# Late modulation columns queued behind their own round's weights, in a transformer kernel on one core

## The chip, the core and the metric

The kernel is one program on one core of a Trainium2 chip. Its engines are TensorE (PE in the profile: matrix products, with PEld for its weight loads), VectorE (DVE), ScalarE (ACT), GpSimd (POOL) and SyncE (SP), which here only issues transfers. Each engine takes its instructions in the order in which they were written into its program; semaphores make it wait for others. The metric is the device time of one execution in microseconds (us); lower is better.

## The reference, cut to what matters

Two transformer blocks run one after the other on 256 tokens of width 1024, all in fp32. The first block ends in a layer that picks among 16,384 single-neuron experts; the second has retention, a Fourier branch and two feed-forward layers. The second block scales and shifts its activations by vectors that come from a small input through one large matrix:

```
mod_x = (silu(c) @ w_ada[l] + b_ada[l])[:, None, :]          # 9 x 1024 outputs, K = 1024
mod_c = (silu(c_ctx) @ w_ada[l] + b_ada[l])[None, None, :]   # the same matrix, another input
...
a = gelu(einsum('bqhkd,bqd->bqhk', peer_u[expert], hb))      # first block: the expert layer
return einsum('bqhk,bqhkd->bqd', g * a, peer_v[expert])
```

In the kernel the expert layer is computed dense: all 128 groups of 128 experts, with a gate that is zero where an expert is not picked.

## The kernel before, in words

Activations lie with the 1024 features in eight chunks of 128 partitions and the 256 tokens along the row. A weight tile is 128x1024 fp32 (512 KB). For fp32 accuracy each tile is split into a high part `wh` (a cast by ACT) and a low part `wl` (a subtraction by DVE, both in `split`, lines 104 and 105), and each product is made of three matmuls (`mm3`, lines 115 to 117).

**The expert stage** is the loop over `i` from 0 to 127, called rounds here. A round does three things. `up(i + 2)` loads a tile of `peer_u`, splits it, multiplies it with `h2` (24 matmuls into `ua`), applies gelu on ACT (`fs`, line 844), multiplies with the gates on DVE (`fs`, line 845) and splits the result into `zh` and `zl` (`two`). `acc_rows` loads a tile of `peer_v`, splits it, and adds 24 matmuls into the accumulators `va`. Then the round may hand out late modulation columns, below. So a clean round is 48 matmuls on PE, two casts and two small operations on ACT, and two `wl` and two small operations on DVE.

The buffers set how far ahead the work runs: four for a loaded tile (`raw`), three each for `wh` and `wl`. `raw_tile` (line 79) issues each load on SP and keeps it in `tmp["dma"]`; `split` keeps its DVE subtraction in `tmp["lo"]`. At the end of a round both are those of the round's `peer_v` tile.

**The late modulation columns** are the 56 tiles of `w_ada_2` that hold outputs 16 to 71 (in chunks of 128) of `mod_x`, 24 of which are wanted for `mod_c` too. `gemv2_late` loads each tile into one of two slots of `gx` and makes a dot product along the row on DVE: one product with `cb2`, and for the 24 tiles a second with `gx[:, 0]`, 80 in all. After every four columns a tiny DVE addition puts the bias on. The generator is pulled in rounds 18 and later by

```
while late and done[0] * 98 < 80 * (i - 17) and next(late, 0) is None:
    pass
```

so that the source has the 80 products spread over rounds 18 to about 115. At round 116 the memory of `gx` is taken over by `hc`.

**What sets the order.** The source order is not the order in the engines' programs: a scheduler places each engine's instructions by its own estimate of when their inputs are ready. Nothing ties a column's load or product to the round that handed it out. `tc.issue_after(ins)` is the tool for that: what is written inside it, as far as it is on the engine of `ins`, is placed behind `ins` in that engine's program; it adds no wait. The kernel uses it elsewhere, as in `some`.

Of the kernel before, what the change touches and what calls it, by code (L numbers as in the profile page):

```python
# [17 lines left out]
OP = mybir.AluOpType  # L18
# [24 lines left out]
def block_kernel(ctx: ExitStack, tc: tile.TileContext, I, out):  # L43
    nc = tc.nc
    V, S, T = nc.vector, nc.scalar, nc.tensor
# [6 lines left out]
    tmp = {"gr": None, "side": 0, "first": 4, "b": 4}  # L52
# [11 lines left out]
    def col(name, i=0, n=1):  # L64
        o, _ = _COLS[name]
        return cols[:, o + i:o + i + n]
# [13 lines left out]
    def raw_tile(src, pool=None):  # L80
        r = (pool or tmp["ws"]).tile([128, 1024], FT, name="raw", tag="raw", bufs=4 if pool else tmp["raw"])
        tmp["dma"] = nc.sync.dma_start(r, src)
        return r
# [236 lines left out]
    def gemv2_late(gx):  # L320

        both, alone = iter(range(16, 40)), iter(range(40, 72))
        for n in range(56):
            i, outs = (next(both), 2) if n % 2 and n < 48 else (next(alone), 1)
            r = gx[:, 2 + n % 2]
            nc.sync.dma_start(r, I["w_ada_2"][i - 16])
            for k, (v, m) in enumerate(((cb2, modx), (gx[:, 0], modc))[:outs]):
                V.scalar_tensor_tensor(r if k == outs - 1 else tmp["gs"], r, 1.0, v, op0=OP.mult, op1=OP.mult,
                                       accum_out=m[:, i:i + 1])
                done[0] += 1  # L330
            if i % 4 == 3:
                s = slice(i - 3, i + 1)
                for m in (modx, modc)[:outs]:
                    V.tensor_add(m[:, s], m[:, s], col("b_ada_2", i - 3, 4))
            yield
# [250 lines left out]
    for c in range(4):  # L586
# [4 lines left out]
        for e in range(2):  # L591
            r = slice(64 * e, 64 * e + 64)
# [256 lines left out]
    with tc.issue_after(tmp["spill"].ins):  # L849
        nc.sync.dma_start(cb2, I["c2"][:, 0])  # L850
        S.activation(cb2, cb2, AF.Silu)
        zs = [up(0), up(1)]
        late = None
        for i in range(128):
            if i < 126:
                zs.append(up(i + 2))
            acc_rows(acc, [I["peer_v"][i]], [zs.pop(0)], i == 0, i == 127)
            if i == 17:

                gx = cr.tile([128, 4, 1024], FT, name="gx", tag="g0")  # L860
                nc.sync.dma_start(gx[:, 0], I["c2"][:, 1])
                S.activation(gx[:, 0], gx[:, 0], AF.Silu)
                tmp["gs"] = gx[:, 1]
                late = gemv2_late(gx)

            while late and done[0] * 98 < 80 * (i - 17) and next(late, 0) is None:
                pass
            if i == 116:
                hch = cr.tile([128, 16, 256], FR, name="hc", tag="g0")
                hch, hcl = hch[:, 0:8], hch[:, 8:16]  # L870
                for k in (0, 4):
                    r = raw_tile(hc_d[:, k:k + 4]).rearrange("p (a b) -> p a b", a=4)
                    split(r, hch[:, k:k + 4], hcl[:, k:k + 4])
                zch = cr.tile([128, 2 * (NF - NFA), 256], FR, name="zc", tag="g1")
                zch, zcl = zch[:, 0:NF - NFA], zch[:, NF - NFA:]
# [415 lines left out]
```

## Time and profile before

| what | value |
|---|---|
| median of 3 runs | 2127.04 us (2125.74 to 2132.92) |
| profiled execution, its own time | 2117.54 us |
| span of the profiled execution, first to last instruction | 2115.6 us |
| mean granted TensorE clock over the span | 0.982 |
| PE busy | 2031.5 us (96%) |
| DVE busy | 1444.3 us (68%) |
| ACT busy | 1050.7 us (50%) |
| HBM read | 403.11 MB |

A matmul record has a start that is taken and an end that is modelled, and matmuls overlap in the pipeline; so "PE busy" hides short gaps, and the number of matmuls that start in a stretch says more about its pace. The expert stage runs from 505.2 us (first `ua` matmul) to 1220 us.

### The profile page before, as it was taken

What the parts mean: (1) busy time and instruction counts of PE and PEld (TensorE: products, weight loads), DVE (VectorE), ACT (ScalarE), POOL (GpSimd) and SP (SyncE); (2) the same over time, 40 slices, a digit from 0 to 9 for tenths busy, and PEclk for the clock granted to TensorE, in tenths of its full rate; (3) what the DMA queues carried; (4) which work ended last, traced back from release to release, by engine and by line L of the source; (5) the groups of instructions that cost most, each with busy time, mean ns of one, the idle gap of its engine ahead of it and who ended that gap; (6) DMA issues with size and microseconds to landing.
All of it is one profiled execution on the core that took longest, in us unless ns stands there. A gap on an engine that the chain in (4) does not pass through costs nothing.

```text
span 2115.6 us, 40439 instructions
## 1 busy us (share of the span) xinstructions
PE 2031.5 (96%) x16326; PEld 1940.6 (92%) x16326; DVE 1444.3 (68%) x2680; ACT 1050.7 (50%) x1745; POOL 136.3 (6%) x92
## 2 busy tenths in 40 slices
PE   6999997899999999999999999999999999999998
PEld 3987897788999999999999999999989899989998
DVE  6876989797589988655556566546734676665555
ACT  3444543498554444454445557534534544444443
POOL 1000176400000000000000000000000000010000
PEclk8999998999999999999999999999999999999999
DMA  9857543214588887655555665534456654434553
GB/s 340 320 175 249 196 154 120 90 41 148 194 288 315 309 290 264 204 192 197 191 198 195 210 233 181 197 112 145 168 182 214 204 175 160 150 137 151 192 196 114
DMA packets 115562, 412.02 MB, mean 195 GB/s; under 512 B 12848, under 2 KB 14384, under 8 KB 114864
## 3 DMA queue, kind: packets, MB, share of 16 engines
q1 hardware_dynamic: 111392, 395.82, 54.2%
q0 software_dynamic: 3696, 13.11, 1.8%
q8 instruction: 128, 2.10, 0.4%
q10 hardware_dynamic: 288, 0.52, 0.1%
q14 instruction: 58, 0.48, 0.1%
HBM read 403.11 MB, written 6.29 MB: 194 GB/s over the span
## 4 chain that ended last, share of the span: by engine, by line
PE 68%; DVE 4%; DMA 3%; ACT 2%; issue 2%; POOL 0%; DVEq 0%; SPq 0%; ACTq 0%; POOLq 0%
PE va L117 5%; PE mm L117 5%; PE va L116 5%; PE ua L117 5%; PE mm L116 5%; PE mm L115 4%; PE ua L115 4%; PE ua L116 4%; PE va L115 4%; PE fu L116 4%; PE fu L115 4%; PE fu L117 4%; DMA gx<-w_ada_dram 3%; PE fa L116 2%; PE fa L117 2%; PE fa L115 2%
## 5 line engine op out<-in xcount | busy, mean ns | idle before, releaser
L105 DVE TENSOR_TENSOR wl<-raw,wh 128x1024 fp32r<-128x1024 f32 x578 | 709.0, 1229 | 493.4 <-ACT wh L104 492.1
L104 ACT CAST wh<-raw 128x1024 fp32r<-128x1024 f32 x614 | 643.5, 1051 | 759.2 <-issue 356.6
L117 PE MATMUL ua<-hh,wl 128*128 128x256 f32 x1024 | 284.3, 278 | 3.6 <-DVE wl L105 3.6
L115 PE MATMUL ua<-hh,wh 128*128 128x256 f32 x1024 | 283.4, 277 | 0.6 <-ACT fs L844 0.3
L116 PE MATMUL ua<-hh,wh 128*128 128x256 f32 x1024 | 283.2, 277 | 0.0
L116 PE MATMUL va<-zl,wh 128*128 128x256 f32 x1024 | 277.8, 278 | 2.9 <-DVE zl L105 2.9
L117 PE MATMUL va<-zh,wl 128*128 128x256 f32 x1024 | 273.6, 278 | 2.0 <-DVE wl L105 2.0
L115 PE MATMUL va<-zh,wh 128*128 128x256 f32 x1024 | 273.1, 277 | 0.0
L116 PE MATMUL mm<-hh,wh 128*128 128x256 f32 x776 | 217.8, 281 | 5.9 <-DVE hh L196 5.8
L115 PE MATMUL mm<-hh,wh 128*128 128x256 f32 x776 | 217.7, 281 | 2.1 <-ACT hh L194 1.4
L117 PE MATMUL mm<-hh,wl 128*128 128x256 f32 x776 | 218.1, 281 | 0.0
L115 PE MATMUL fu<-hh,wh 128*128 128x256 f32 x704 | 196.3, 280 | 2.8 <-ACT hh L199 1.6
L117 PEld LDWEIGHTS ua<-hh,wl 128*128 128x128 f32 x1024 | 192.3, 188 | 5.6 <-DVE wl L105 5.6
L116 PE MATMUL fu<-hh,wh 128*128 128x256 f32 x704 | 196.1, 279 | 0.9 <-DVE hh L200 0.9
L117 PE MATMUL fu<-hh,wl 128*128 128x256 f32 x704 | 195.8, 278 | 0.0
L116 PEld LDWEIGHTS va<-zl,wh 128*128 128x128 f32 x1024 | 191.7, 189 | 3.4 <-DVE zl L105 3.3
L115 PEld LDWEIGHTS ua<-hh,wh 128*128 128x128 f32 x1024 | 192.5, 188 | 1.0 <-ACT fs L844 0.5
L116 PEld LDWEIGHTS ua<-hh,wh 128*128 128x128 f32 x1024 | 192.3, 188 | 0.0
L117 PEld LDWEIGHTS va<-zh,wl 128*128 128x128 f32 x1024 | 189.0, 189 | 2.9 <-DVE wl L105 2.8
L115 PEld LDWEIGHTS va<-zh,wh 128*128 128x128 f32 x1024 | 189.3, 189 | 0.0
L116 PEld LDWEIGHTS mm<-hh,wh 128*128 128x128 f32 x776 | 146.8, 189 | 7.2 <-DVE hh L196 6.7
L115 PEld LDWEIGHTS mm<-hh,wh 128*128 128x128 f32 x776 | 147.3, 190 | 4.5 <-ACT hh L194 1.5
(415 smaller groups left out, 4559.3 us busy)
## 6 DMA issues: line engine op xcount, KB each, us to landing
raw<-w_ffn_dram SPq DMA_DIRECT2D x177, 512.0 KB, 3.4
raw<-peer_u_dram SPq DMA_DIRECT2D x128, 512.0 KB, 4.3
raw<-peer_v_dram SPq DMA_DIRECT2D x128, 512.0 KB, 4.2
gx<-w_ada_dram SPq DMA_DIRECT2D x56, 512.0 KB, 5.0
raw<-w_ada_dram SPq DMA_DIRECT2D x40, 512.0 KB, 6.3
raw<-w_in_2v_dram SPq DMA_DIRECT2D x32, 512.0 KB, 3.3
raw<-w_in_dram SPq DMA_DIRECT2D x25, 512.0 KB, 4.5
raw<-w_out_dram SPq DMA_DIRECT2D x16, 512.0 KB, 3.2
```

What stands on the lines that cost most here:

```text
L104: S.copy(hi, src)
L105: tmp["lo"] = eng.tensor_sub(lo, src, hi.bitcast(FT))
L115: T.matmul(o, lh, rh, start=start, stop=False, **kw)
L116: T.matmul(o, lh, rl, start=False, stop=False, **kw)
L117: tmp["mm"] = T.matmul(o, ll, rh, start=False, stop=stop, **kw)
```

## The change: a column's transfer is placed behind the load, its products behind the low part, of the round's last weights

Two `issue_after` blocks are put around the two kinds of instructions of a column. The transfer is placed on SP behind the last weight load that the source has issued, and each product on DVE behind the last `wl` that it has issued; both are those of the round's `peer_v` tile. The bias additions are left free.

```diff
             r = gx[:, 2 + n % 2]
-            nc.sync.dma_start(r, I["w_ada_2"][i - 16])
+
+            with tc.issue_after(tmp["dma"].ins):
+                nc.sync.dma_start(r, I["w_ada_2"][i - 16])
             for k, (v, m) in enumerate(((cb2, modx), (gx[:, 0], modc))[:outs]):
-                V.scalar_tensor_tensor(r if k == outs - 1 else tmp["gs"], r, 1.0, v, op0=OP.mult, op1=OP.mult,
-                                       accum_out=m[:, i:i + 1])
+                with tc.issue_after(tmp["lo"].ins):
+                    V.scalar_tensor_tensor(r if k == outs - 1 else tmp["gs"], r, 1.0, v, op0=OP.mult, op1=OP.mult,
+                                           accum_out=m[:, i:i + 1])
```

On SP, this is the program before at the place where the first columns are loaded (`raw` are weight tiles, `gx<-w_ada_dram` are columns, `gx<-c_dram` is the input of `mod_c`):

```order
L861 DMA gx<-c_dram 128x1024
L326 DMA gx<-w_ada_dram 128x1024 x2
L82 DMA raw<-peer_u_dram 128x1024
L82 DMA raw<-peer_v_dram 128x1024
L326 DMA gx<-w_ada_dram 128x1024
L82 DMA raw<-peer_u_dram 128x1024
L82 DMA raw<-peer_v_dram 128x1024
L326 DMA gx<-w_ada_dram 128x1024 x2
L82 DMA raw<-peer_u_dram 128x1024
```

And this is the same place with the change:

```order
L864 DMA gx<-c_dram 128x1024
L82 DMA raw<-peer_u_dram 128x1024
L82 DMA raw<-peer_v_dram 128x1024
L82 DMA raw<-peer_u_dram 128x1024
L82 DMA raw<-peer_v_dram 128x1024
L328 DMA gx<-w_ada_dram 128x1024
L82 DMA raw<-peer_u_dram 128x1024
L82 DMA raw<-peer_v_dram 128x1024
L328 DMA gx<-w_ada_dram 128x1024
L82 DMA raw<-peer_u_dram 128x1024
```

Before, five columns stand among the next five weight loads; now a column always stands behind a `peer_v` load, at most one to a round. Before, the last column's load stands some 60 rounds into the stage; now the columns reach to round 115 of its 128.

On DVE, this is the program before around the fourth addition to `modc` (`modx<-gx,cb` is a column's product for `mod_x`, `modc<-gx` the second product; `wl`, `fs` and `zl` are the stage's own work):

```order
L105 TENSOR_TENSOR wl<-raw,wh 128x1024
L334 TENSOR_TENSOR modc<-modc,cols 128x4
L328 SCALAR_TENSOR_TENSOR gx,modx<-gx,cb_5459 128x1024
L105 TENSOR_TENSOR wl<-raw,wh 128x1024
L845 TENSOR_TENSOR fs<-fs,gall_4364 128x256
L328 SCALAR_TENSOR_TENSOR gx,modx<-gx,cb_5459 128x1024
L105 TENSOR_TENSOR zl<-fs,zh 128x256
L105 TENSOR_TENSOR wl<-raw,wh 128x1024
L105 TENSOR_TENSOR zl<-fs,zh 128x256
L328 SCALAR_TENSOR_TENSOR gx,modc<-gx 128x1024
L328 SCALAR_TENSOR_TENSOR gx,modx<-gx,cb_5459 128x1024
L105 TENSOR_TENSOR wl<-raw,wh 128x1024
```

And this is a stretch behind the same addition with the change:

```order
L105 TENSOR_TENSOR zl<-fs,zh 128x256
L105 TENSOR_TENSOR wl<-raw,wh 128x1024
L848 TENSOR_TENSOR fs<-fs,gall_4364 128x256
L105 TENSOR_TENSOR wl<-raw,wh 128x1024
L105 TENSOR_TENSOR zl<-fs,zh 128x256
L105 TENSOR_TENSOR wl<-raw,wh 128x1024
L331 SCALAR_TENSOR_TENSOR gx,modx<-gx,cb_5459 128x1024
L848 TENSOR_TENSOR fs<-fs,gall_4364 128x256
L331 SCALAR_TENSOR_TENSOR gx,modc<-gx 128x1024
L105 TENSOR_TENSOR wl<-raw,wh 128x1024
L105 TENSOR_TENSOR zl<-fs,zh 128x256
L105 TENSOR_TENSOR wl<-raw,wh 128x1024
```

Before, up to three products stood between one `fs` and the next; now a round (`fs wl zl wl`) takes at most one. The second product of a column that has two stands behind the next round's `fs`. Every engine has the same instructions as before; outside the expert stage their order is unchanged.

## Rows read from the trace of the kernel before

**Rows 1.** The page: busy time by engine; DMA share in 40 slices

```profile
PE 2031.5 (96%) x16326; PEld 1940.6 (92%) x16326; DVE 1444.3 (68%) x2680; ACT 1050.7 (50%) x1745; POOL 136.3 (6%) x92
...
DMA  9857543214588887655555665534456654434553
```

**Rows 2.** Sums by stretch: PE, PEld, DVE, ACT, POOL busy (records), clock, DMA

```profile
513.00:590.00 77.00, 77.00 (x681) 77.00 (x680) 44.40 (x58) 38.65 (x60) 0.00 (x0) 1.00 0.60 202
590.00:846.00 256.00, 248.29 (x2116) 245.31 (x2115) 223.92 (x358) 123.63 (x180) 0.00 (x0) 0.99 0.86 297
850.00:1106.00 256.00, 256.00 (x2261) 256.00 (x2260) 147.29 (x190) 126.38 (x189) 0.00 (x0) 1.00 0.57 196
```

**Rows 3.** Everything that touches the tile gx: count, min/median/max ns, first and last start

```profile
L326 SPq DMA_DIRECT2D gx<-w_ada_dram x56: 327/328/656, 589.5 to 840.1; - x56
L328 DVE SCALAR_TENSOR_TENSOR gx<-gx,cb x56: 1215/1224/1228, 597.1 to 844.4; 128x1024 f32<-128x1024 f32 x56
...
L328 DVE SCALAR_TENSOR_TENSOR gx<-gx x24: 1214/1219/1222, 602.0 to 823.5; 128x1024 f32<-128x1024 f32 x24
...
DMA to landing us min/median/max: 3.1/5.0/8.4
```

**Rows 4.** Waits from 590 to 845 us: total us, times, longest

```profile
ACT zh L104 <- DVE fs L845: 57.0, 33, 3.5
DVE gx L328 <- DMA gx<-w_ada_dram: 30.8, 24, 2.8
```

**Rows 5.** DVE's timeline at 759 us: start, duration, instruction, [idle before]

```profile
759.09 1.23 DVE L328 SCALAR_TENSOR_TENSOR gx<-gx,cb 128x1024 f32<-128x1024 f32 x1 [2.49 <-DMA gx<-w_ada_dram]
...
760.24 1.22 DVE L105 TENSOR_TENSOR wl<-raw,wh 128x1024 fp32r<-128x1024 f32 x1
...
762.85 0.42 DVE L105 TENSOR_TENSOR zl<-fs,zh 128x256 fp32r<-128x256 f32 x1
```

**Rows 6.** PE's timeline, two of its stalls

```profile
621.32 0.39 PE L117 MATMUL va<-zh,wl 128*128 128x256 f32 x1 [1.09 <-DVE wl L105]
...
763.33 0.38 PE L116 MATMUL va<-zl,wh 128*128 128x256 f32 x1 [2.32 <-DVE zl L105]
```

**Rows 7.** Sums behind the second stall: PE busy (records), granted clock, DMA

```profile
763.90:767.50 3.60, 3.60 (x20) 0.53 0.79 251
```

**Rows 8.** The same sums for a stretch in the crowd and one behind it

```profile
624.00:693.00 69.00, 68.62 (x578) 1.00 0.89 313
850.00:919.00 69.00, 69.00 (x611) 1.00 0.59 199
```

**Rows 9.** Timeline of one clean round, all engines

```profile
848.94 1.23 DVE L105 TENSOR_TENSOR wl<-raw,wh 128x1024 fp32r<-128x1024 f32 x1
...
850.15 0.28 PE L115 MATMUL ua<-hh,wh 128*128 128x256 f32 x1
...
850.19 0.33 SPq L82 DMA_DIRECT2D raw<-peer_v_dram  x1
...
850.28 1.06 ACT L104 CAST wh<-raw 128x1024 fp32r<-128x1024 f32 x1 [1.09 <-issue]
...
851.36 1.23 DVE L105 TENSOR_TENSOR wl<-raw,wh 128x1024 fp32r<-128x1024 f32 x1 [0.86 <-ACT wh L104]
...
852.87 0.28 PE L115 MATMUL va<-zh,wh 128*128 128x256 f32 x1
...
855.22 0.42 DVE L845 TENSOR_TENSOR fs<-fs,gall 128x256 f32<-128x256 f32 x1
...
855.59 0.28 PE L115 MATMUL ua<-hh,wh 128*128 128x256 f32 x1
...
856.80 1.23 DVE L105 TENSOR_TENSOR wl<-raw,wh 128x1024 fp32r<-128x1024 f32 x1 [1.16 <-ACT wh L104]
```

**Rows 10.** DMA issues from 850 to 1150 us: KB each, median us to landing

```profile
raw<-peer_v_dram SPq DMA_DIRECT2D x56, 512.0 KB, 3.3
```

**Rows 11.** SP's own waits from 590 to 845 us: total us, times, longest

```profile
SPq L326 <- DVE gx L328: 52.6, 36, 4.4
```

## The prediction

> **What bounds the kernel now.** First the page: PE is busy for 96% of the span and DVE for 68% [rows 1], so what can be won is PE's lost time, and one looks for a stretch where it loses some. The slices of DMA point to one: from the twelfth to the fifteenth slice (about 580 to 790 us) the share is 8, and it goes down to 5 behind them [rows 1]. The sums by stretch say what PE does there. In the 256 us from 590 to 846, 2116 matmuls ran; in an equal stretch right behind it, of the same loop, 2261, and PE was never idle [rows 2]. One clean matmul takes 256 / 2261 = 0.1132 us, and a clean round of 48 takes 5.44. So the stretch (the crowd, below) is short of 145 matmuls, or 145 x 0.1132 = 16.4 us. Before the stretch there is nothing to win either: 513 to 590 has PE busy all the time [rows 2].
>
> The view of the tile gx tells what is different: all 56 late columns are loaded and multiplied from 589.5 to 845.6 us, though the source hands them out over 98 rounds, more than twice as long [rows 3]. So DVE has 80 products more, and is busy for 223.92 of 256 us, with DMA at 297 instead of 196 GB/s [rows 2]. To that come 30.8 us in which DVE stood waiting for a column to land, in 24 waits of up to 2.8 us [rows 4]. Together 254.7 of 256 us: DVE has nothing left, and the subtraction that makes `wl` and `zl` comes late to PE. The timeline shows one case from end to end. DVE waits 2.49 us for a column, with the `wl` of the next weights queued behind it; product, `wl`, another product, and only at 762.85 the `zl` [rows 5]. PE has waited 2.32 us for that `zl` [rows 6]. Then the granted clock is at its lower level, 1.2 instead of 2.4 GHz, for nearly all of 3.6 us, in which 20 matmuls run where 31.8 would have [rows 7].
>
> What the 16.4 us are made of: PE idle 256 - 248.29 = 7.7 [rows 2]; the clock 11.8 x 0.1132 = 1.3 [rows 7]; a slower step from 624 to 693 us, where 578 matmuls stand against 611 [rows 8], 33 x 0.1132 = 3.7, of which 0.4 is idle and counted, leaves 3.3; the other 4.1 are gaps that the modelled ends cover.
>
> **The change part by part.** Nothing is removed or added; the listings show the same instructions on every engine, and another order in the expert stage alone.
>
> The *transfers* move behind the `peer_v` load of their round. How early is that? SP issues a `peer_v` load at 850.19, right when the `wl` that frees its slot has ended (848.94 + 1.23 = 850.17) [rows 9]. With four `raw` slots, that tile's own `wl` is four weights later: a weight is 24 matmuls, 2.72 us (850.15, 852.87 and 855.59 are the starts of three in a row), so it begins about 859.8 and ends at 861.0 [rows 9]. The column's transfer, issued 0.33 later, has from 850.5 to 861.0, 10.5 us. Landing took 5.0 at the median in the crowd and 8.4 at most [rows 3]; weights outside it take 3.3 [rows 10]. So no product should wait for its transfer, where 24 did; I take 0 us. If landing took over 10.5 us, rival 1 follows. The load on DMA becomes 196 GB/s plus 56 x 0.524 MB in 97 rounds of 5.44 us, 56 GB/s: about 252, an estimate from [rows 2], against 297 in the crowd.
>
> The *products* move behind the `wl` of their round, at most one to a round; the second one of 24 columns comes behind the next round's `fs`. In DVE's queue a product takes 760.24 - 759.09 = 1.15 us [rows 5]. A clean round leaves DVE idle twice, 0.86 and 1.16 us, both waiting for the cast [rows 9]: 2.0 for 1.15, plus an addition of four columns now and then. The average need is 80 x 1.15 / 98 = 0.94. So DVE no longer runs out of time; what is left to see is lateness within a round. A product behind the `wl` that ends about 855.3 in that round would hold `fs` from 855.22 to about 856.5; `fs` ends near 856.9, and the `wl` of 856.80 starts 0.1 late [rows 9]. With a second product behind `fs` it starts at about 858.0, 1.2 late. How much lateness is covered? The cast at 850.28 starts once a third weight back has left its buffer (850.15); its `wl` runs from 851.36 to 852.59, and the weight is wanted two weights on, at 855.59: 3.0 us of cover [rows 9]. 1.2 is less than 3.0. So the cost is 0; if the cover were gone, it would be the lateness of 24 rounds, 24 x 1.2 = 29 us at most, and below nothing it can't be, since PE has no idle time in those rounds to give back.
>
> What is *late next* on the queues passed: on SP a column may wait for its slot, until the product of the column before the last is done. Those stand two to four rounds apart, so at the closest it waits for one product, 1.15 us, and holds the next `peer_u` load, which has about the same 10.5 us to land in. On ACT, `zh` waits for `fs`; it did so for 57.0 us in the crowd [rows 4], and now by at most 1.2 in a round, of which the casts behind it, spaced by PE, feel nothing. The columns that end last are wanted only in the second block.
>
> The *sum*: -16.4 + 0 + 0. The profiled execution took 2117.54 us, 1.9 more than its span; it would become 2101.1. The median of the runs shown, 2127.04, is 9.5 above that execution; the gain does not depend on that, so I forecast 2127.04 - 16.4 = 2110.6.
>
> **The rivals.** What a measurement of this kernel can tell from no change is about 0.3%, 6.4 us.
>
> 1. *The columns still hold the queues: no change.* SP takes its issues in order, so a column that waits for its slot holds the weights behind it; in the crowd SP waited 52.6 us so, at most 4.4 [rows 11]. 4.4 of waiting and 8.4 of landing are 12.8, over 10.5 by 2.3; if that came for 24 columns, as the 24 waits did [rows 4], DVE would again stand for some 30 us and PE lose about what it lost: 2127. Against it: those 4.4 were waits for products in a full DVE queue, which goes. The Trainium skill has this as a rule, in "DMA: Bandwidth & Descriptors", section "Anatomy of one DMA": a DMA engine itself waits for no semaphore, the issuing sequencer waits before it hands the transfer on. By that rule, which speaks against placing columns between weights, every slot wait is paid by the weights behind it; the trace agrees on the wait's place [rows 11].
>
> 2. *A stall early on leaves PE in its slower step: slower.* From 621 to 693 us PE hardly waited and yet needed (69 - 0.38) / 578 = 0.1187 us a matmul, against 69 / 611 = 0.1129 [rows 8]; this came right behind a stall [rows 6] and lasted until others. That is 48 x 0.0058 = 0.28 us a round. If one stall by the first products (round 18) set it, and no later one ended it, 110 rounds would pay 30.6: 2127 - 16.4 + 30.6 = 2141. It decides from 16.4 / 0.28 = 59 rounds on. Against it: without stalls the step stayed clean, before the crowd and behind it [rows 2], and the cover says that there is no stall.
>
> 3. *A part of the gain.* The second products make `wl` later than I worked out, by 0.3 us over the cover in each of 24 rounds: 7 us given back, 2118.
>
> That the change doesn't do what it says is ruled out by the listings; that the crowd is not the cause is ruled out by the 850 us mark, where PE's loss ends with the last column.
>
> **How the numbers follow.** Chances: the whole gain 0.66, part of it (rival 3) 0.12, no change (rival 1) 0.15, slower (rival 2) 0.07. Faster by over 0.3% are the first two, 0.78; within 0.3% 0.15; slower 0.07. The prediction is that of the first, 2110.6. The low end is the profiled execution less the whole gain, 2101, since nothing outside the stretch can be won. The high end, 2124, is rival 3's 2118 and on top of it what the highest run shown stands above the median, 5.9; left out are most of rivals 1 and 2.
>
> **What would show it.** In the changed profile the products should run from about 605 to 1135 us, DVE's wait for columns be near 0, the 256 us from 590 hold about 2261 matmuls with no clock below the upper level, DMA near 250 GB/s up to 1135, and the last `ua` matmul come 16 us sooner. A wait of DVE for `gx`, PE waits for `wl` or `zl` in rounds with two products, or 578 instead of 611 matmuls in 69 us without waits would make it wrong, and name the rival.

## The result, and the profile after

The changed kernel takes 2104.56 us at the median of 4 runs (2102.91 to 2109.76); the kernel before, beside it, 2129.98 (2125.74 to 2136.26, 4 runs). The medians are 25.4 us apart, 1.2%; the ratio of the runs is put at 0.9869, with an interval from 0.9828 to 0.9909, so the gain is small but clear of the spread. The forecast was 16.4 us less, 2110.6 with a range of 2101 to 2124. Medians below are of all runs, but ratios leave out an execution that was more than 1.5% above the fastest of its kernel, which takes out three of the ten with the transfers' edge alone.

The page of the changed kernel, the lines that answer to [rows 1]:

```profile
PE 2037.0 (97%) x16326; PEld 1947.2 (92%) x16326; DVE 1448.6 (69%) x2680; ACT 1054.8 (50%) x1745; POOL 137.4 (7%) x92
...
DMA  9857553213677676777777655534556655444553
```

The 8s of the DMA line are gone; a plateau of 6 and 7 reaches to the 23rd slice. Next its sums by stretch (us, then busy time and records of PE, PEld, DVE, ACT, POOL, clock, DMA share, GB/s), to be laid beside [rows 2]:

```profile
513.00:590.00 77.00, 77.00 (x679) 76.80 (x679) 45.00 (x60) 38.88 (x60) 0.00 (x0) 1.00 0.60 201
590.00:846.00 256.00, 256.00 (x2261) 256.00 (x2261) 187.56 (x272) 132.50 (x192) 0.00 (x0) 1.00 0.71 247
850.00:1106.00 256.00, 256.00 (x2261) 256.00 (x2261) 191.12 (x277) 129.25 (x188) 0.00 (x0) 1.00 0.73 249
```

From 590 to 846 us PE starts 2261 matmuls where it started 2116, the number of a clean stretch, and the clock's 0.99 is 1.00. DVE's 223.92 us are 187.56, and the next stretch, which had none of the products and 147.29 us, has 191.12. The tile gx, as in [rows 3], and the waits of 590 to 1140 us, as in [rows 4]; the waits are an answer of their own, so a second fence:

```profile
L328 SPq DMA_DIRECT2D gx<-w_ada_dram x56: 327/427/1527, 601.1 to 1124.1; - x56
...
L331 DVE SCALAR_TENSOR_TENSOR gx<-gx,cb x56: 1217/1218/1221, 611.5 to 1133.7; 128x1024 f32<-128x1024 f32 x56
...
L331 DVE SCALAR_TENSOR_TENSOR gx<-gx x24: 1218/1219/1221, 618.6 to 1075.3; 128x1024 f32<-128x1024 f32 x24
...
DMA to landing us min/median/max: 4.2/5.3/6.8
```

```profile
DVE wl L105 <- ACT wh L104: 140.6, 122, 2.0
...
ACT zh L104 <- DVE fs L848: 0.3, 1, 0.3
```

DVE's wait for a column (30.8 us in 24 waits before) is no longer in the list at all, and ACT's wait for `fs` fell from 57.0 to 0.3 us. What DVE waits for now is the cast, as it should in a clean round. The timeline of one round with a product, on DVE:

```profile
865.99 1.23 DVE L105 TENSOR_TENSOR wl<-raw,wh 128x1024 fp32r<-128x1024 f32 x1 [1.15 <-ACT wh L104]
867.13 1.22 DVE L331 SCALAR_TENSOR_TENSOR gx<-gx,cb 128x1024 f32<-128x1024 f32 x1
...
868.27 0.42 DVE L848 TENSOR_TENSOR fs<-fs,gall 128x256 f32<-128x256 f32 x1
868.72 1.23 DVE L105 TENSOR_TENSOR wl<-raw,wh 128x1024 fp32r<-128x1024 f32 x1
...
871.43 1.23 DVE L105 TENSOR_TENSOR wl<-raw,wh 128x1024 fp32r<-128x1024 f32 x1 [1.15 <-ACT wh L104]
```

The product takes 868.27 - 867.13 = 1.14 us of the queue and `fs` comes behind it; the next `wl` starts 2.73 us after the last one, and the one behind it 2.71, the pace of PE's weights. In place of DVE's wait of 1.15 us stands a product, and nothing is late.

**Where the 25 us are.** In the two profiled executions the last `va` matmul moved from 1220.0 us, the stage's end before, to 1204.7:

```profile
L117 PE MATMUL va<-zh,wl x1024: 275/277/281, 519.3 to 1204.7; 128*128 128x256 f32 x171
```

The stage, from the first `ua` matmul, is 505.4 to 1204.7 = 699.3 us against 505.2 to 1220.0 = 714.8: 15.5 less. But the profiled execution of the changed kernel is the slowest of its four (2109.76 us, span 2107.8), and that of before was faster than all four timed ones (2117.54, span 2115.6). Their spans differ by 7.8 us only: behind the stage the changed kernel took 2107.8 - 1204.7 = 903.1 us, before 2115.6 - 1220.0 = 895.6. The sums on PE (PE's busy time and records, granted clock, DMA share, GB/s), for 69 us out of the stage and 69 out of the first feed-forward layer, show how. Of the changed kernel:

```profile
850.00:919.00 69.00, 69.00 (x611) 1.00 0.73 249
...
1300.00:1369.00 69.00, 69.00 (x589) 1.00 0.52 172
```

and of the kernel before:

```profile
1300.00:1369.00 69.00, 69.00 (x611) 1.00 0.59 201
```

The feed-forward ran at 69 / 589 = 0.1171 us a matmul in one execution and at 0.1129 in the other, both with a busy PE and the full clock. In 190 us of that layer 1616 matmuls start against 1679, and 63 x 0.113 = 7.1 is nearly all of the 7.5 us. That is the slower step of the prediction's second rival, in a place that the change doesn't touch. The step is the time from one matmul's start to the next; this one is called the long step below, and the other the short one. (A count also holds the two or three matmuls that only reach into its stretch, so a quotient from 69 us comes out some 0.4% low: stretches of 380 and 400 us below give 0.1132 and 0.1177.)

### The profile page after: what moved, and what is told of

The parts are those of the page before. It is cut to its first block, busy times and chain, and to the rows that moved or that the text cites. A ratio compares the mean times of both kernels' runs of the same rounds, so it can differ in the third digit from the quotient of the medians.

```text
span 2107.8 us, 40413 instructions
## 1 busy us (share of the span) xinstructions
PE 2037.0 (97%) x16326; PEld 1947.2 (92%) x16326; DVE 1448.6 (69%) x2680; ACT 1054.8 (50%) x1745; POOL 137.4 (7%) x92
## 4 chain that ended last, share of the span: by engine, by line
PE 74%; ACT 2%; DVE 2%; issue 0%; DVEq 0%; ACTq 0%
PE ua L117 6%; PE ua L115 6%; PE ua L116 6%; PE va L116 6%; PE va L117 6%; PE va L115 6%; PE mm L117 5%; PE mm L116 5%; PE mm L115 5%; PE fu L115 4%; PE fu L116 4%; PE fu L117 4%; PE fa L116 2%; PE fa L117 2%; PE fa L115 2%; ACT o L828 1%
## 5 line engine op out<-in xcount | busy, mean ns | idle before, releaser
L105 DVE TENSOR_TENSOR wl<-raw,wh 128x1024 fp32r<-128x1024 f32 x578 | 709.4, 1229 | 509.4 <-ACT wh L104 505.2
L116 PE MATMUL va<-zl,wh 128*128 128x256 f32 x1024 | 282.8, 277 | 0.0
L117 PE MATMUL va<-zh,wl 128*128 128x256 f32 x1024 | 282.4, 277 | 0.0
L115 PE MATMUL va<-zh,wh 128*128 128x256 f32 x1024 | 281.9, 276 | 0.0
L115 PE MATMUL fu<-hh,wh 128*128 128x256 f32 x704 | 198.4, 283 | 2.7 <-ACT hh L199 1.5
L116 PE MATMUL fu<-hh,wh 128*128 128x256 f32 x704 | 198.3, 282 | 0.9 <-DVE hh L200 0.9
```

What stands on the lines that cost most here:

```text
L105: tmp["lo"] = eng.tensor_sub(lo, src, hi.bitcast(FT))
L115: T.matmul(o, lh, rh, start=start, stop=False, **kw)
L116: T.matmul(o, lh, rl, start=False, stop=False, **kw)
L117: tmp["mm"] = T.matmul(o, ll, rh, start=False, stop=stop, **kw)
```

## The experiments

Times of before are those taken on the same chip beside each group of kernels.

**One edge alone.** The first kernel keeps the transfer's edge and drops the products'; the second does the reverse.

```diff
-                with tc.issue_after(tmp["lo"].ins):
-                    V.scalar_tensor_tensor(...)
+                V.scalar_tensor_tensor(...)
```

> The kernel before, with the transfers alone placed behind their round's weight loads; the products are placed freely. In the listing this spreads the products as well (at most one to a round, up to round 115), since a product can't stand ahead of its transfer. My theory (the loss is DVE out of time in the crowd, its queue held by columns that have not landed): the expert stage, first to last of its matmuls, is 699 us as with the whole change (714.7 before), DVE never waits for a column, and the kernel takes 0.985 to 0.992 of before. Rival (the product's place behind wl matters by itself): DVE waits for columns, since a product may stand ahead of its round's wl, and the stage lies between 703 and 715 us.

```diff
-            with tc.issue_after(tmp["dma"].ins):
-                nc.sync.dma_start(r, I["w_ada_2"][i - 16])
+            nc.sync.dma_start(r, I["w_ada_2"][i - 16])
```

> The kernel before, with the products alone placed behind their round's wl; the transfers are placed freely. In the listing the two slots of gx then hold the transfers back too, so they stand two or three weight loads earlier than with the whole change. My theory: the stage is 699 us, DVE never waits for a column, 0.985 to 0.992 of before. Rival (a column that is queued early on SP waits for its slot and holds the weight loads behind it): SP waits for the slots by several us each, ACT waits for weights to land, and the stage is over 703 us.

Transfers alone: 2122.29 us (2102.24 to 2144.37, 10 runs) against 2128.31, 6.0 less, ratio 0.9929 (0.9887 to 0.9972). The stage of its profiled execution is 706.4 us long, where 699 was expected and 703 to 715 by the rival. Its products are spread as well (605.7 to 1133.2 us), but they stand earlier in DVE's queue than in the changed kernel (the first at 605.7 us, not 611.5), and DVE comes to them before their columns have landed. From the list of waits of 590 to 1212 us, and the sums of two stretches:

```profile
ACT zh L104 <- DVE fs L846: 71.4, 54, 2.9
DVE gx L329 <- DMA gx<-w_ada_dram: 54.5, 42, 2.7
```

```profile
1078.00:1147.00 69.00, 69.00 (x589) 69.00 (x588) 47.93 (x69) 33.67 (x49) 0.00 (x0) 1.00 0.77 258
936.00:1005.00 69.00, 69.00 (x611) 69.00 (x611) 52.20 (x77) 35.02 (x51) 0.00 (x0) 1.00 0.73 247
```

DVE waits more than before, 54.5 us, though it was expected to wait for no column, and PE still hardly stalls, since outside the crowd DVE has time to catch up. PE's one real stall, 0.62 us for a `wl` at 1076.69, is followed by the long step to the end of the stage; the long step also stood from 1036 to 1059 us. So in this execution a spread of the transfers wasn't the change's whole worth, and the place of the products mattered; the intervals of the two ratios overlap, so the times alone don't show it.

Products alone: 2099.93 us (2098.92 to 2128.23, 4 runs), ratio 0.9898 (0.9821 to 0.9974). The four runs are 2098.92, 2098.94, 2100.93 and 2128.23, so it can't be told from the full change; the stage is 698.2 us long, as expected. Here columns are issued freely and the tile gx shows no wait of DVE for one. SP's own waits from 590 to 1200 us:

```profile
SPq L326 <- DVE gx L329: 40.7, 18, 2.3
SPq L326 <- DVE fs L846: 32.3, 29, 1.1
SPq L326 <- DVE modx L335: 15.2, 7, 2.4
```

88.2 us of waits of columns in SP's queue, with weights behind them, and 2262 matmuls in the 256 us from 590: that hold, the first rival's mechanism, cost nothing here, as the weights are loaded far enough ahead: ACT waited 2.5 us in all for one to land.

**Half a crowd.** Both kernels keep before's order. The first loads 16 of 1024 values of each column, with zeros in the rest of the slot, and makes full products, all of them into the scratch row; the second loads whole columns and multiplies 16 values. So each leaves out most of the modulation.

```diff
-            nc.sync.dma_start(r, I["w_ada_2"][i - 16])
+            nc.sync.dma_start(r[:, 0:16], I["w_ada_2"][i - 16][:, 0:16])
...
-                V.scalar_tensor_tensor(r if k == outs - 1 else tmp["gs"], ...)
+                V.scalar_tensor_tensor(tmp["gs"], ...)
...
+                nc.gpsimd.memset(gx[:, 2:4], 0.0)
```

> The kernel before, but a column's transfer moves 16 of its 1024 columns (8 KB), the rest of the slot being zero, and every product writes to the scratch row; so the 80 products come in a crowd without the load on DMA and without long waits for landings. It leaves out most of the modulation weights. In the listing the crowd has 1.6 products a round, rounds 17 to about 66. DVE's need is then about 3.3 + 1.6 x 1.15 = 5.1 of 5.44 us a round. My theory (products and waits for landings together exhaust DVE): without the waits DVE just suffices, and the stage loses under 4 of its 15 us (under 703). Rival A (products alone exhaust DVE): the stage stays above 710. Rival B (the load on DMA is what costs): under 701.

```diff
-                V.scalar_tensor_tensor(r if k == outs - 1 else tmp["gs"], r, 1.0, v, ...)
+                V.scalar_tensor_tensor(r[:, 0:16] if k == outs - 1 else tmp["gs"][:, 0:16], r[:, 0:16], 1.0,
+                                       v[:, 0:16], ...)
```

> The kernel before, but each product covers 16 of the 1024 columns of its tile, so DVE's work for the columns is nearly nothing, while all 29 MB still come in a crowd. It leaves out most of each product. My theory: DVE waits for columns that have not landed, 20 us or more in sum, but with its time otherwise free it catches up within the 3.0 us of cover, and the stage loses under 4 us (under 703). Rival B (the load on DMA is what costs, by late weights): the stage stays above 708, with ACT waiting for weights to land for over 10 us. Rival C (the waits for landings alone are enough): the stage stays above 708, with PE waiting for wl and zl behind waits of DVE for gx.

Products crowded, 2109.78 us; transfers crowded, 2100.42 (one run each). The sums from 590 to 846 us, of the first and then of the second, with the second's waits for columns:

```profile
590.00:846.00 256.00, 256.00 (x2262) 256.00 (x2261) 235.32 (x373) 130.26 (x191) 0.00 (x0) 1.00 0.60 198
```

```profile
590.00:846.00 256.00, 256.00 (x2261) 256.00 (x2261) 158.98 (x373) 130.32 (x191) 0.00 (x0) 1.00 0.86 311
```

```profile
DVE gx L328 <- DMA gx<-w_ada_dram: 40.0, 36, 2.4
```

The first has DVE busy for 235.32 us, more than before; the second has before's load on DMA, and more waits of DVE for columns than before (40.0 us against 30.8). In both PE runs the clean 2261 or 2262. Before had 223.92 of work and 30.8 of waits, 254.7 of 256, and of the three only that cost PE anything. The first run alone would also fit a loss by the load on DMA, since that went too (198 GB/s); the second, with 311 GB/s, rules out that load by itself. (The first one's 2109.78 holds a second feed-forward layer at the long step; its stage was 698.4 us long, the second's 699.3.)

**Doubled products.** Each product is made twice, in the changed kernel's places, to see how much cover there is; then three times.

```diff
+                    for _ in range(1):     # 2 in the other
+                        V.scalar_tensor_tensor(tmp["gs"], r, 1.0, v, op0=OP.mult, op1=OP.mult,
+                                               accum_out=tmp["xs"])
...
+    tmp["xs"] = work.tile([128, 1], FT, name="xs", tag="xs")
```

> The changed kernel with every product made twice (160 products, the extra ones into scratch, behind the same wl). DVE's need rises by 0.94 to about 3.3 + 1.9 = 5.2 of 5.44 us a round, and two products in one round can make the next wl late by 2.3 us, under the 3.0 us of cover. My theory (PE loses only when DVE is out of time or later than the cover): no stall of PE, expert stage under 702 us. Rival (what counts is that a round has at most one product): PE waits for wl or zl in many rounds, stage over 708.

> The changed kernel with every product made three times (240). DVE's need is 3.3 + 0.82 x 3 x 1.15 = 6.1 us a round against 5.44, over 98 rounds 65 us too much. My theory: DVE is busy all the time and sets the pace, and the stage is 699 + 65 = 764 us, 745 to 780 with what the buffers absorb. Rival (PE's time is set by something other than DVE's time, such as transfers): under 720.

2166.82 and 2205.96 us (one run each), and not for the reason tested: the doubled kernel has no stall of PE from 521 us to the stage's end, but a longer step everywhere, ahead of the first product too:

```profile
521.00:590.00 69.00, 69.00 (x584) 1.00 0.57 186
...
2050.00:2119.00 69.00, 69.00 (x584) 1.00 0.56 184
```

The new 4-byte tile had moved the weight tiles up by 64 bytes. So neither run says what a product costs. The tripled one has that longer step too, and its stage of 738.7 us missed the 745 to 780 that were expected, because its products ran on behind the stage's end, to 1267 us; it is not used further. The doubled one was made again with the scratch inside a tile that is there for padding, so that every other tile stays where it was:

```diff
-    wp.tile([128, 64], FT, name="pad0")
+    tmp["xs"] = wp.tile([128, 64], FT, name="pad0")[:, 0:1]
```

> The changed kernel with every product made twice, the extra results into the padding tile, all tiles at the changed kernel's addresses (the first version of this had them moved, and its rounds took 5.7 us for that reason, so that it did not test the cover). DVE's need is 5.2 of 5.44 us a round. My theory (PE waits only when wl is later than 3.0 us of cover): no wait of PE for wl or zl from 590 to 1200 us, stage under 702 us if PE keeps the short step. Rival (at most one product a round is needed): PE waits for wl or zl in tens of rounds, stage over 708.

2104.48 us (one run), the changed kernel's time. Its sums:

```profile
590.00:846.00 256.00, 256.00 (x2261) 256.00 (x2260) 225.88 (x344) 132.84 (x192) 0.00 (x0) 1.00 0.70 247
850.00:1106.00 256.00, 256.00 (x2262) 256.00 (x2261) 232.59 (x355) 129.35 (x188) 0.00 (x0) 1.00 0.72 247
```

DVE is busy for 225.88 and 232.59 of 256 us, more than the crowd's 223.92, with 160 products placed behind their rounds' weights over some 525 us, and it never waits for a column. PE loses nothing. So behind the weights DVE has room for products about as dense as in the crowd (80 in 256 us), as long as it doesn't also wait for columns.

**The kernel before again**, unchanged, for a second profile of it.

> The kernel before once more, for a second profile of it: its runs spread over 20 us, and the profiled one was the shortest of all. If the longer step explains the spread and the gain beyond 16.4 us, this profile shows the crowd again (some 16 us lost to waits and longer steps from 590 to 846), and, if its time is over 2120, further stretches at 0.118 us a matmul behind the last column or in the two feed-forward stages. If the spread has another source, the stretches outside the crowd are at 0.113 us, and the longer time stands elsewhere.

2139.01 us, span 2137.0: 21.4 more than the first profile. The stage ends at 1238.9 and is 733.7 us long, 18.9 of the 21.4. Sums on PE:

```profile
514.00:630.00 116.00, 116.00 (x988) 1.00 0.68 228
646.30:688.00 41.70, 41.70 (x354) 1.00 0.92 317
...
767.00:780.00 13.00, 13.00 (x117) 1.00 0.85 283
780.60:813.60 33.00, 33.00 (x281) 1.00 0.80 267
815.00:828.00 13.00, 13.00 (x117) 1.00 0.80 276
830.00:1230.00 400.00, 400.00 (x3399) 1.00 0.60 196
```

And the same sums of the first profile of before:

```profile
642.50:693.00 50.50, 50.50 (x428) 1.00 0.89 317
...
767.60:810.00 42.40, 42.40 (x376) 1.00 0.79 275
...
830.00:1210.00 380.00, 380.00 (x3356) 1.00 0.59 203
```

Between stalls a stretch keeps one step: 41.7 / 354 = 0.1178 us, 33 / 281 = 0.1174 (long), 42.4 / 376 = 0.1128 (short). The step changes at the stalls, some of them too short to be listed as waits, and the last one leaves its step to all that follows. In the second profile that is this one, in PE's timeline:

```profile
829.51 0.38 PE L117 MATMUL va<-zh,wl 128*128 128x256 f32 x1 [0.75 <-DVE wl L105]
```

Behind it 400 / 3399 = 0.1177 us a matmul to the stage's end; behind the last stall of the first profile (825.99 us) 380 / 3356 = 0.1132. Over the 409 us from 830 to 1239 that is 409 x (1 - 0.1132 / 0.1177) = 15.6 of the 18.9 us. (Of the other 3.3 us, 2.6 were lost ahead of 630 us: from 505 us on 1040 matmuls start there against 1063 in the first profile, 23 x 0.1132, with 514 to 630 at the long step.)

**One stall put in.** A reduction that takes 5.48 us on DVE, behind the third column's product of the changed kernel, makes PE wait once, to see whether one stall sets the step of the rounds behind it. The first attempt used the 4-byte tile, the second the place in the padding tile.

```diff
+                if n == 2:
+                    with tc.issue_after(tmp["lo"].ins):
+                        V.tensor_reduce(tmp["xs"], gall[2][:, 0:20], axis=AX.XY, op=OP.max)
```

> The changed kernel with one DVE reduction of 5120 elements, about 5.4 us, put once behind the third column's product (round 21), its result unused. It makes one wl late by over 4 us, against 3.0 us of cover, so PE should stall once for 1 to 3 us and never again in the stage. Theory of the longer step (rival 2 of the prediction: PE that has once caught up with its inputs goes on at 0.118 instead of 0.113 us a matmul until something resets it): behind the stall the matmuls of a 69 us stretch are about 587 instead of 611, for hundreds of us, and the stage is up to 25 us longer; if it is chance whether a stall leaves PE so, the timed runs fall into two groups some 20 us apart. Rival (the longer step comes from the crowd's load on DVE or DMA): the stage is 701 us, 611 matmuls in 69 us behind the stall, and the time is that of the changed kernel plus 2 us.

> The one-stall kernel again (a 5.4 us DVE reduction once, behind the third column's product), but its result goes into a padding tile that is there anyway, so that every tile stands at the addresses of the changed kernel; in the first one-stall kernel a new tile had moved the weight tiles by 64 bytes, and the whole program, ahead of the stall too, ran at 0.119 us a matmul. Theory (a stall draws anew whether PE goes on at the short or the longer step, and it stays so until the next stall): up to the stall 611 matmuls in 69 us; behind it either 611 or about 588 to the end of the stage; the timed runs spread over some 25 us more than those of the changed kernel, in groups near 2102 and 2127. Rival (one stall costs its own length): all runs within 2100 to 2112, 611 matmuls in 69 us behind it.

The first took 2169.1 us (2168.35 to 2173.11, 4 runs; ratio 1.0197, 1.0115 to 1.0280), but with a longer step from 521 us on (584 matmuls in 69 us), ahead of its stall: the moved tiles again, and no answer. The second took 2111.58 us (2109.69 to 2112.97, 4 runs; before 2140.47; ratio 0.9881, 0.9819 to 0.9942). Its stage is 701.6 us long, 2.3 more than the changed kernel's, and its runs lie within 3.3 us of each other, where two groups near 2102 and 2127 were expected: by the time alone it is much as the rival has it (2100 to 2112), and a stall costs its own length. PE's timeline says more. The one reduction made two stalls:

```profile
632.75 0.28 PE L115 MATMUL ua<-hh,wh 128*128 128x256 f32 x1
632.87 0.28 PE L116 MATMUL ua<-hh,wh 128*128 128x256 f32 x1
633.94 0.39 PE L115 MATMUL ua<-hh,wh 128*128 128x256 f32 x1 [0.79 <-ACT wh L104]
...
635.32 0.28 PE L115 MATMUL ua<-hh,wh 128*128 128x256 f32 x1
...
637.68 0.28 PE L117 MATMUL ua<-hh,wl 128*128 128x256 f32 x1
638.85 0.38 PE L117 MATMUL ua<-hh,wl 128*128 128x256 f32 x1 [0.90 <-DVE wl L105]
```

From 635.32 to 637.68 stand 20 steps, 0.118 us each. Ahead of the first stall and behind the second the step is short:

```profile
521.00:590.00 69.00, 69.00 (x611) 1.00 0.56 192
640.00:709.00 69.00, 69.00 (x611) 1.00 0.72 253
```

So the first stall did bring the long step, and the second, 5 us later, took it away before it could cost anything.

**Other places in memory.** The weight tiles, and with them what is laid out behind them in memory, are moved by the size of the padding tile alone, with every engine's instructions as in the changed kernel.

```diff
-    wp.tile([128, 64], FT, name="pad0")
+    wp.tile([128, 48], FT, name="pad0")     # 96 in the other
```

> The changed kernel with a padding tile 64 bytes smaller, so that the weight tiles stand 64 bytes lower against the activations; every engine's program is the same, instruction for instruction. Theory (the step depends on where weights and activations stand in the memory relative to each other): the share of the program at the longer step changes, in either direction: all of it at 0.118 or more (about 2165 us, as with 64 bytes higher), or less of it than in the changed kernel (about 2080 to 2098 us). Rival (place does not matter): 2099 to 2110 us, as the changed kernel.

> The same with the padding tile 128 bytes larger, one step of 64 bytes beyond the place at which the whole program ran at 0.119 us a matmul (2164 to 2169 us). Theory (place): not that of the changed kernel; if what counts repeats every 128 bytes, as the changed kernel (2099 to 2110), if not, the whole program at the longer step (2150 or more) or at the short one (2080 to 2098). Rival (the longer step of the three moved kernels came from their additional instructions, not from the place): 2099 to 2110 us with PE at the longer step only behind stalls.

64 bytes lower: 2181.76 us (2180.51 to 2182.57, 4 runs), ratio 1.0210 (1.0147 to 1.0273) to before. 128 bytes higher: 2153.3 (nine runs from 2149.57 to 2154.9, and one of 2127.95), ratio 1.0055 (1.0018 to 1.0091). Sums on PE of the first, then of the second:

```profile
521.00:590.00 69.00, 69.00 (x578) 1.00 0.55 190
...
2050.00:2119.00 69.00, 69.00 (x578) 1.00 0.55 183
```

```profile
521.00:590.00 69.00, 69.00 (x589) 1.00 0.55 188
...
2050.00:2119.00 69.00, 69.00 (x588) 1.00 0.56 187
```

With nothing but the place changed, the whole program, in the profiled executions, runs at 0.1194 or 0.1172 us a matmul and is 77 or 49 us longer than the changed kernel (2181.76 and 2153.3 less 2104.56; beside them the doubled kernel at the old place took 2104.48).

## Why the prediction was right, and where its size was off

**What bounds the kernel.** Right, and shown from both sides, in one run each: a crowd of products alone or of transfers alone leaves PE its 2261 matmuls; only both together used up DVE's time.

**The transfers.** 10.5 us to land were worked out; landing took 6.8 at most, and no product waited. 252 GB/s were estimated; 247 and 249 were measured. Sharing the stage with the columns did not slow PE.

**The products.** 1.15 us of the queue became 1.14; the `wl` behind a product, forecast 0.1 us late, was on time within 0.02. The cover held behind the columns with two products, as no wait of PE shows, and held with every product doubled. Which of the two edges does it was not part of the prediction: the products' edge is enough.

**What is late next.** A column's wait for its slot was bounded at 1.15 us: SP waited 4.5 us in 4 such waits, 1.1 at most.

**The first rival** needed SP's holds to make the weights late. In the kernel with the products' edge alone they came to 88.2 us, 2.4 at most, and cost nothing. Its own price doesn't add up either: 2.3 us over the 10.5 in 24 columns is 55 us, and the 30 were taken over from [rows 4]. What the Trainium skill states in "DMA: Bandwidth & Descriptors", section "Anatomy of one DMA — SWDGE (gpsimd) path", that the issuing sequencer does the waiting, agrees with these rows; the loss that was feared from it did not come.

**The sum in its own terms.** Of the profiled execution 16.4 us were to go. The stage became 15.5 shorter, and 145 matmuls are back in their 256 us; the missing 0.9 lies ahead of the crowd, where 8 matmuls are missing, 6 of them at the stage's start. There the granted clock was 0.79 in the changed kernel and 1.00 before (the first line is of the changed kernel):

```profile
505.00:513.00 8.00, 6.98 (x45) 0.79 0.93 323
```

```profile
505.00:513.00 8.00, 6.69 (x51) 1.00 0.92 315
```

In the changed kernel it was at its lower level, 1.2 GHz, for 3.4 us from 507 us on (0.51 granted), behind 2 us in which PE was busy for 0.98 only. The change has no part in that: the second profile of the kernel before has 0.79 and 45 matmuls there as well.

**What was sized wrong is the step from that execution to the median**: "the median of the runs shown, 2127.04, is 9.5 above that execution; the gain does not depend on that". It does. That profile shows the cheaper ending: its last stall in the crowd left the short step, so that the slower step cost 3.3 us, within the crowd [rows 8]. In the second profile the last stall left the long one, and the stage had 733.7 - 699.3 = 34.4 us to give back. The measured 25.4 (2129.98 - 2104.56) lie between 15.5 and 34.4; that the timed runs are a mix of such endings fits, but only two executions were traced, so it is argued and not shown. Of the 13 runs of before beside the last kernels, two took 2117 and 2119 us and eleven 2135 to 2150, as two endings would have it; the 13 beside the first kernels are spread from 2121 to 2142 without such a gap. Taking all that lies above the profiled execution, 16.4 + 9.5 = 25.9, would have come nearer, but that it comes so near is in part luck, since the changed kernel has long steps of its own, in the feed-forward. The range held the result because its low end, 2101, was worked out from the profiled execution and not from the median.

**The second rival** had the mechanism right, that a stall can set a longer step for all rounds behind it, and put it on the wrong kernel: in the crowd of before, PE's waits for `wl` and `zl` number 12 in the first profile and 7 in the second; the changed kernel has none from 514 us to the stage's end. It was given 30.6 us for 110 rounds, 0.28 a round; the one such ending that was traced cost 15.6 in the 72 behind the last stall, 0.22 a round, because the 0.1187 of [rows 8] holds short gaps besides the long step's 0.1177. The 2128.23 us among the products' runs may be the long step over a whole stage (699 x (1 - 0.1132 / 0.1177) = 27 us by these rows, where it is 29.3 above the lowest); that run has no trace.

## What to carry to other kernels

Before work is moved, add an engine's busy time and its waits by stretch: here neither a queue that was 92% busy nor one that waited for loads was a loss by itself, but the two together left nothing over. Tie the instruction that holds up others to the one whose turn it is, here the product to the last weight's subtraction; a load that stood early in its queue then did no harm here. When executions of one program differ by more than the effect, profile it twice and compare counts of matmuls in equal stretches, and give a test kernel its scratch where no other tile moves.

## What the runs showed of the hardware that was not expected

At this kernel's place in memory a stream of these matmuls has a step of 0.1132 or of 0.1177 us at the full granted clock and with PE shown as busy throughout, 611 or 588 in 69 us. The step was drawn anew at restarts behind a gap and mostly kept until the next one. The gap can be too short to be listed as a wait: at 702.7 us of the second profile of before, two starts that lie 0.18 us apart, where 0.11 is usual, are followed by the long step. One change came without any gap, at 1036.6 us of the kernel with the transfers' edge alone; what made it, and what decides a draw, is open.

A move of the weight tiles by 64 or 128 bytes changed the step of the whole program: the same instructions took 2104.56, 2153.3 or 2181.76 us, and 4 bytes of scratch put into the wrong pool cost 62 us (2166.82 against 2104.48 with doubled products). Smaller moves, and how weights and moving data have to lie to each other, were not tried.
